# Fourier stage of a diffusion layer: four places for the prompt's output tiles, and the put-off sums, the first level's sums and the last level's halving at other places in the order

## The chip, the cores and the metric

The kernel runs on one core of a Trainium2 chip. The metric is the device time of one execution in microseconds. TensorE (PE) multiplies, VectorE (DVE), ScalarE (ACT) and GpSimd (POOL) do the elementwise work, and DMA transfers are issued from the queues of SyncE (SP) and GpSimd. The profile also gives the clock that TensorE was granted, as a share of full speed.

## The reference, cut to what matters

One layer of a diffusion backbone, in float32, for two streams: a prompt of 256 tokens and a latent of 2048 tokens, both with 1024 channels. The part that the change touches is the Fourier mixing of 512 of the projected channels, in four groups of 128:

```python
def project(h, w_in, q_g, k_g):
    p = h @ w_in
    q, k, v, f = jnp.split(p, [QK_WIDTH, 2 * QK_WIDTH, 2 * QK_WIDTH + ATTN_WIDTH], axis=-1)
    ...
    f = f.reshape(b, n, N_FOUR_GROUPS, FOUR_GROUP)
    return q, k, v, f

def fourier_mix(f, w_four):
    b, n, _, _ = f.shape
    spec = jnp.fft.fft2(f.astype(jnp.float32), axes=(1, 3), norm='ortho').real.astype(f.dtype)
    return jnp.einsum('bngc,gce->bnge', spec, w_four).reshape(b, n, FOUR_WIDTH)

def merge(attn, four, subln_g, lam_init, w_out):
    ...
    return jnp.concatenate([a.reshape(b, n, ATTN_WIDTH), four], axis=-1) @ w_out
```

Around it stand a normed and modulated projection, differential attention over 2560 keys, the output projection and a squared-ReLU MLP.

## The kernel before

The stages follow each other on one core: modulation vectors, the projection of all 18 token blocks (16 latent ones, two of the prompt), the Fourier stage, attention, output projection, MLP. The Fourier stage stands in the block `c2`, whose order of instructions is written out by hand (`tc.manual_schedule()`): each engine gets its instructions in the order in which the code issues them.

**How the transform is split.** Positions are 2048 rows. The projection already leaves sums and differences of row r and row r + 1024 in DRAM. The 2048-point transform is split by halves: the differences give the odd output columns (the level with the names E, DR and "o"), and the eight tiles `SS` of 128 rows hold the sums, 1024 rows. The level of 1024 folds these again: `diff` (L791) writes the difference of tile t and tile t + 4 to `d`, `summed` (L794) adds in place. Each set of differences is split into an even and an odd part by `even_odd`: two matmuls with a reversing matrix (`reverse`, L805 and L807) put the mirrored rows in PSUM, and VectorE writes `e` = d - mirror (L815) and `o` = d + mirror (L816); one row of the first `o` tile is overwritten by a copy (L818). Each product then takes half of the cosine or sine matrix. The same happens once more with 512 rows (`fold(512, t)`: L791, then L794), and the last 256 rows are halved by `s_last` (L781, L782).

**The levels and groups.** For each level the products run over the four channel groups g = 0 to 3: "o" (2048), then "p" (the prompt's 256 rows), "e" (1024), "f" (512) and "l" (256). Group g of a level makes two products A and B (`ab`, L744; `ab_half`, L752; for "o" `ab2048`, L732), each evacuated by ScalarE (L736 or L754). One group later `yT` multiplies A and B with the group's map: `py` (L698) and `pz` (L700) in PSUM, ScalarE copies py to `yu` (L704), and VectorE writes yu - pz and yu + pz to the output columns and their mirror image (L712, L713). Outputs of the latent stream gather in four tiles `ys` of 128 x 2048, one for each group (named ys_4656 to ys_4659 in the order below), stored by L773 after the last level; the prompt's go to tiles `yp` of 128 x 256, stored by L762. Both stores are issued from GpSimd's queue.

**The put-off sums.** At the 2048 level the output has a further split by parity: for group g, `yd` = u - v (L716) and u = u + v (L717) on VectorE, then four half-width results, two on GpSimd (L719, L720) and two on VectorE (L721, L722). Group 0 does this at once. For the groups 1 to 3 these six instructions are put in the list `LATE`, with copies of both products, and each `late()` issues those of the next group.

**The order.** The table `AFTER` says what is issued after group g of a level. PSUM tiles of the tag "y" (py, pz and rev) share three places, those of the tag "ab" five; a matmul that writes one waits for the readers of the tile that had the place before. `yp`, `d`, `yu` and `yd` come from the pool `f_t` with two or four places for a tag; `yp` has two. The pools are handed on tile by tile, so attention's first loads (keys L965, queries L993, values L971, all on SP's queue) go out as soon as the tiles of the Fourier stage that lay in their place are released.

Attention starts with score products (L1019), whose maxima VectorE takes (L1024) before ScalarE's exponentials. GpSimd starts it with a memset (L938), then scales and subtracts the two exponentials (L1058, L1059), which TensorE transposes (L1074).

Of the kernel before, what the change touches and what calls it, by code (L numbers as in the profile page):

```python
# [11 lines left out]
F32 = mybir.dt.float32  # L12
# [7 lines left out]
P = 128  # L20
D = 1024
KD = D // P
NP = 256
# [18 lines left out]
def body(tc, a, out):  # L42
    nc = tc.nc
    ctx = ExitStack()
    with ctx:
# [184 lines left out]
        with ExitStack() as c1:  # L230
# [357 lines left out]
            V = nc.vector  # L588
            with tc.manual_schedule():
# [12 lines left out]
                def ft32(pool, tag, nm, bufs):  # L602
                    return pool.tile([P, 512], F32, tag=tag, name=nm, bufs=bufs)
# [30 lines left out]
                SS = []  # L634
# [51 lines left out]
        with ExitStack() as c2:  # L686
            ft = c2.enter_context(tc.tile_pool(name="f_t", bufs=2, reuse_waits="tile"))
            yp = c2.enter_context(tc.tile_pool(name="f_y", bufs=1, reuse_waits="tile"))
            fw = c2.enter_context(tc.tile_pool(name="f_w", bufs=1, side="right", reuse_waits="tile"))
# [4 lines left out]
            def yT(dst, g, A, B, w, mirror_dst, parity=False):  # L694

                r = cw[g]
                py = pp.tile([P, 512], F32, tag="y", name="py", bufs=3)
                nc.tensor.matmul(py[:, :w], r[:, 0, :], A[:, :w], start=True, stop=True)  # L698
                pz = pp.tile([P, 512], F32, tag="y", name="pz", bufs=3)
                nc.tensor.matmul(pz[:, :w], r[:, 1, :], B[:, :w], start=True, stop=True)  # L700

                late = w == 512 and g > 0
                u, v = ft.tile([P, 512], F32, tag="yl" if late else "yu", name="yu", bufs=3 if late else 2)[:, :w], pz[:, :w]
                nc.scalar.copy(u, py[:, :w])  # L704
                if late:
                    v = ft.tile([P, 512], F32, tag="yv", name="yv", bufs=3)
                    nc.scalar.copy(v, pz)

                def go():
                    if not parity:  # L710
                        c = slice(1, P) if w == HW else slice(0, w)
                        V.tensor_sub(dst, u, v)  # L712
                        V.tensor_add(mirror_dst, u[:, c], v[:, c])  # L713
                        return
                    d = ft.tile([P, 512], F32, tag="yd", name="yd", bufs=2)
                    V.tensor_sub(d, u, v)  # L716
                    V.tensor_add(u, u, v)  # L717
                    de, do, se, so_ = d[:, 0:256], d[:, 256:512], u[:, 0:256], u[:, 256:512]
                    nc.gpsimd.tensor_add(dst[:, 0:256], de, do)  # L719
                    nc.gpsimd.tensor_sub(mirror_dst[:, 511:255:-1], de, do)  # L720
                    V.tensor_sub(dst[:, 511:255:-1], se, so_)  # L721
                    V.tensor_add(mirror_dst[:, 0:256], se, so_)  # L722

                LATE.append(go) if late else go()
# [32 lines left out]
            HW = P + 1  # L757

            def put_prompt(g, A, B):
                y = ft.tile([P, NP], F32, tag="yp", name=f"yp{g}")  # L760
                yT(y[:, 0:HW], g, A, B, HW, y[:, NP - 1:P:-1])
                nc.gpsimd.dma_start(four[g * P:g * P + P, 0:NP], y)  # L762

# [27 lines left out]
                V.tensor_sub(d[t], SS[t], SS[t + n // 2 // P])  # L791

            def summed(n, t):
                V.tensor_add(SS[t], SS[t], SS[t + n // 2 // P])  # L794

            def fold(n, t):
                diff(n, t)
                summed(n, t)
# [3 lines left out]
            def reverse(n, t):  # L802
                d, T = DD[n], n // P // 2
                REV[n, t] = ps = pp.tile([P, 512], F32, tag="y", name=f"rev{n}_{t}", bufs=3)
                nc.tensor.matmul(ps, jm, d[2 * T - 1 - t], start=True, stop=t == 0)  # L805
                if t:
                    nc.tensor.matmul(ps, k0, d[2 * T - t], start=False, stop=True)  # L807

            def even_odd(n, t):

                if (n, t) not in REV:
                    reverse(n, t)
                d, T, ps = DD[n], n // P // 2, REV.pop((n, t))
                e, o = (ft32(fa, "src", f"{x}{n}_{t}", 12) for x in "eo")
                V.tensor_sub(e, d[t], ps)  # L815
                V.tensor_add(o, d[t], ps)  # L816
                if t == 0:
                    nc.scalar.copy(o[0:1, :], d[T][0:1, :])  # L818
                for x, y in zip("eo", (e, o)):
                    EO.setdefault((n, x), []).append(y)  # L820

# [7 lines left out]
            def late():  # L829
                LATE.pop(0)()  # L830

            AFTER = {("o", 1): [(s_prompt,), (load_mats, "c1024", "s1024", "c512", "s512")],
                     ("o", 3): [(diff, 1024, 3), (diff, 1024, 2), (diff, 1024, 0), (diff, 1024, 1)],
                     ("p", 0): [(reverse, 512, 0), (even_odd, 512, 0)], ("p", 1): [(reverse, 512, 1), (even_odd, 512, 1)],
                     ("p", 3): [(summed, 1024, 0), (summed, 1024, 2)],
                     ("e", 0): [(summed, 1024, 1), (summed, 1024, 3), (fold, 512, 0)], ("e", 1): [(fold, 512, 1), (late,)],
                     ("e", 2): [(reverse, 256, 0), (s_last,), (late,)], ("e", 3): [(even_odd, 256, 0)],
                     ("f", 1): [(late,)]}

            def after(*at_):  # L840
                for fn, *args in AFTER.get(at_, ()):
# [7 lines left out]
            with tc.manual_schedule():  # L849
# [55 lines left out]
                for n, (ea, ma, eb, mb), w, p in (  # L905
                        ("p", (None, "c256", None, "s256"), HW, put_prompt),
                        ("e", (lambda: EO[512, "e"], "c1024", lambda: EO[512, "o"], "s1024"), 256, put(1024)),
                        ("f", (lambda: EO[256, "e"], "c512", lambda: EO[256, "o"], "s512"), 128, put(512)),
                        ("l", (None, "c256", None, "s256"), HW, put(256))):
                    for g in range(4):  # L910
                        if n in "pl":
                            nA, nB = (ab_half(g, q, (PR, S3)[n == "l"], MT[m][0], n) for q, m in enumerate((ma, mb)))
                        else:
                            nA = ab(g, 0, ea(), MT[ma], w, n)
                            nB = ab(g, 1, eb(), MT[mb], w, n)
                        last_put(*pend)
                        last_put, pend = p, (g, nA, nB)
                        if n == "p" and g == 0:
                            k_store(0, NK[0] // P - 1, parts[0])
                        if n == "e" and g == 0:  # L920
                            q_store(LAST, parts[1])
                        after(n, g)
# [8 lines left out]
        with ExitStack() as c3_:  # L931
# [265 lines left out]
            T = TSTEP  # L1197
# [692 lines left out]
        with ExitStack() as c6:  # L1890
# [52 lines left out]
            for i in range(7):  # L1943
                for k in range(16):
                    n = i * 16 + k
# [7 lines left out]
            with tc.manual_schedule():  # L1953
                pend, NM, loaded, KS = None, 7 * 24, 4, []
                for i in range(7):
                    for b in range(3):
                        ps = [pp.tile([P, 512], F32, tag="ps", name=f"ps{i}_{b}_{j}", bufs=6) for j in range(3)]
                        for k in range(16):
                            n, m = i * 16 + k, (i * 3 + b) * 8 + k // 2
# [35 lines left out]
                for j in range(3):  # L1995
                    t = 6 + j
# [70 lines left out]
```

## Time and profile before

| what | value |
|---|---|
| time, median of 3 runs | 2900.94 us (2899.92 to 2901.82) |
| profiled execution, its own time | 2899.16 us |
| its span in the trace | 2897.0 us |
| VectorE, share of the span | 69% |
| ScalarE | 53% |
| GpSimd | 36% |
| DMA traffic, mean | 170 GB/s |

Sums made from the trace are to be compared with the profiled execution's own time and not with the median. A row of a timeline gives the start, the duration of one instruction and its engine, line, operation and tiles (buffer numbers left out), and in brackets how long the engine was idle before and what ended that. Instructions alike and next to each other are put together (x2, x4), with their times together. Windows give the busy time of every engine in a stretch, then the clock granted to TensorE (1.00 is full speed) and the share and rate of the DMA engines.

### The profile page before, as it was taken

The page shows a single profiled execution, that of the slowest core. Times are in us where ns is not written, and L with a number is a line of the kernel's source. Part 1 is how long each engine was busy: PE and PEld are TensorE (multiplying, and loading weights), DVE is VectorE, ACT ScalarE, POOL GpSimd, SP SyncE. Part 2 cuts the span into 40 slices and gives each one's busy share as a digit, 9 for nine tenths or more (in the row PEclk, how much of TensorE's full clock was granted, in tenths as well). Part 3 has the DMA queues.
Part 4 walks back from the last instruction along what each step waited for, and adds up shares of the span by engine and source line. Part 5 has one row for each costly group of instructions (what it writes and reads, how often), then busy time and mean ns, then how long its engine had stood idle before and what let it go on. Part 6 is the DMA issues. An engine that isn't in the chain of part 4 may idle for free.

```text
span 2897.0 us, 43205 instructions
## 1 busy us (share of the span) xinstructions
PE 2850.3 (98%) x15119; PEld 2470.4 (85%) x15119; DVE 2011.4 (69%) x3377; ACT 1547.0 (53%) x3504; POOL 1057.0 (36%) x866
## 2 busy tenths in 40 slices
PE   8999999799999999999999999999999999999999
PEld 4888788588888888888889999999998888888887
DVE  6667776798988988964477777778775354345554
ACT  4333323598998989953356565556554332233221
POOL 1112112499998999942213333333332000000000
PEclk9999999999999999999999999999999999999999
DMA  7777888420121202136777677667657464445663
GB/s 282 206 201 189 229 214 228 182 102 28 48 110 44 104 30 74 60 101 200 225 240 227 210 254 230 213 230 233 225 178 251 139 200 138 138 142 180 201 207 109
DMA packets 392779, 492.93 MB, mean 170 GB/s; under 512 B 26467, under 2 KB 306384, under 8 KB 389490
## 3 DMA queue, kind: packets, MB, share of 16 engines
q1 hardware_dynamic: 387136, 479.73, 52.4%
q0 software_dynamic: 1872, 7.28, 0.8%
q10 hardware_dynamic: 3554, 3.17, 0.4%
q8 instruction: 119, 1.95, 0.3%
q14 instruction: 98, 0.80, 0.1%
HBM read 312.58 MB, written 179.59 MB: 170 GB/s over the span
## 4 chain that ended last, share of the span: by engine, by line
PE 89%; DVE 4%; DMA 3%; ACT 2%; issue 1%; POOL 1%; SPq 0%; ACTq 0%; DVEq 0%; POOLq 0%
PE Ss L1019 10%; PE ps L88 8%; PE ps L89 8%; PE ps L90 8%; PE pts L1074 5%; PE po L90 4%; PE po L88 4%; PE po L89 4%; PE pj L88 4%; PE pj L89 4%; PE pj L90 4%; PE pA L1682 2%; PE pA L1683 2%; PE pB L1683 2%; PE pB L1682 2%; PE pB L1684 2%
## 5 line engine op out<-in xcount | busy, mean ns | idle before, releaser
L1024 DVE TENSOR_REDUCE mxs<-Ss 128x1 f32<-128x512 f32 x636 | 413.0, 684 | 64.7 <-PE Ss L1019 52.9
L1359 DVE TENSOR_TENSOR sl<-sr,sh 128x768 fp32r<-128x768 f32 x168 | 161.7, 963 | 338.0 <-ACT sh L1358 336.4
L1059 POOL TENSOR_TENSOR P0s<-P0s,P1s 128x1024 f32<-128x1024 f32 (+2 forms) x128 | 378.5, 2957 | 10.7
L1358 ACT CAST sh<-sr 128x768 fp32r<-128x768 f32 x168 | 140.2, 835 | 424.8 <-PE ps L89 422.0
L1724 POOL TENSOR_TENSOR gs<-g,g 128x384 f32<-128x384 f32 x48 | 69.6, 1451 | 469.5 <-ACT g L1694 399.9
L1043 ACT ACTIVATE P1s<-Ss,mxs 128x512 f32<-128x512 f32 x318 | 215.2, 694 | 36.4 <-DVE mxs L1027 35.4
L88 PE MATMUL pj<-wh,hh 128*128 128x512 f32 x576 | 228.9, 397 | 4.5 <-DVE qn L289 3.9
L89 PE MATMUL ps<-tlT,sh 128*128 128x512 f32 x585 | 229.3, 392 | 0.0
L88 PE MATMUL ps<-thT,sh 128*128 128x512 f32 x585 | 229.0, 391 | 0.0
L89 PE MATMUL pj<-wl,hh 128*128 128x512 f32 x576 | 227.4, 395 | 0.5 <-DVE wl L524 0.5
L90 PE MATMUL ps<-thT,sl 128*128 128x512 f32 x585 | 227.7, 389 | 0.0
L90 PE MATMUL pj<-wh,hl 128*128 128x512 f32 x576 | 226.7, 394 | 0.0
L1043 ACT ACTIVATE P0s<-Ss,mxs 128x512 f32<-128x512 f32 x318 | 214.1, 691 | 5.5 <-DVE mxs L1027 4.8
L1019 PE MATMUL Ss<-KS1s,Qs 128*128 128x512 f32 x636 | 195.9, 420 | 5.0 <-ACT P0s L1043 2.4
L1019 PE MATMUL Ss<-KS0s,Qs 128*128 128x512 f32 x636 | 196.8, 422 | 2.4 <-ACT P1s L1043 2.4
L1074 PEld LDWEIGHTS pts<-ident,P0s 128*128 128x128 f32 x1280 | 158.2, 140 | 44.2 <-POOL P0s L1059 1.4
L1074 PE MATMUL pts<-ident,P0s 128*128 128x128 f32 x1280 | 191.3, 273 | 1.9 <-POOL P0s L1059 1.2
L1693 ACT ACTIVATE g<-uz 128x384 f32<-128x384 f32 x144 | 75.8, 527 | 201.6 <-DVE uz L1716 171.4
L1058 POOL TENSOR_SCALAR P1s<-P1s,tots 128x1024 f32<-128x1024 f32 (+2 forms) x128 | 171.8, 1342 | 5.8
L1086 DVE TENSOR_TENSOR als<-pts,ahs 128x512 fp32r<-128x512 f32 x256 | 165.8, 680 | 6.9 <-ACT ahs L1081 6.6
L88 PE MATMUL ps<-ophT,sh 128*128 128x512 f32 x423 | 165.8, 392 | 1.1 <-DVE uz L1716 1.1
L90 PE MATMUL ps<-ophT,sl 128*128 128x512 f32 x423 | 165.7, 392 | 0.0
(530 smaller groups left out, 8055.7 us busy)
## 6 DMA issues: line engine op xcount, KB each, us to landing
sr<-sd SPq DMA_DIRECT2D x84, 768.0 KB
a<-in_w SPq DMA_DIRECT2D x184, 256.0 KB
sd<-gs SPq DMA_DIRECT2D x192, 192.0 KB
sd<-g SPq DMA_DIRECT2D x144, 192.0 KB
wm<-in_w_mod SPq DMA_DIRECT2D x32, 512.0 KB
Qs<-qd SPq DMA_DIRECT2D x32, 512.0 KB
b<-in_w SPq DMA_DIRECT2D x64, 256.0 KB
b<-tsum SPq DMA_DIRECT2D x64, 256.0 KB
```

The source lines that it names most:

```text
L88: nc.tensor.matmul(ps, lh, rh, start=first, stop=False)
L89: nc.tensor.matmul(ps, lh, rl, start=False, stop=False)
L90: nc.tensor.matmul(ps, ll, rh, start=False, stop=last)
L1019: nc.tensor.matmul(S[:, :w], self.Q[:, x, m, j * P:j * P + P], self.hd.KS[m][:, b * 512:b * 512 + w], start=(x == 0), stop=(x == 1))
L1024: nc.vector.tensor_reduce(self.mx[j][:, m, b:b + 1], self.S[j, m, b], axis=AX.X, op=ALU.max)
L1043: nc.scalar.activation(dst, S, AF.Exp, bias=self.mx[j][:, m, 6:7], accum_out=self.sm[j][:, m, b:b + 1])
L1058: nc.gpsimd.tensor_scalar(p, p, tot[:, 3:4], 0.0, op0=ALU.mult, op1=ALU.add)
L1059: nc.gpsimd.tensor_add(d, d, p)
L1074: nc.tensor.transpose(pt[:, c:c + P], self.p0[j][:, (kb + t) * P:(kb + t + 1) * P], ident)
L1086: nc.vector.tensor_sub(t, self.pt[kb], f32(self.A[kb][0]))
L1358: nc.scalar.copy(hi, src)
L1359: nc.vector.tensor_sub(lo, src, f32(hi))
```

## The change

It has five parts. The prompt's output tiles `yp` come from the pool `f_w`, on the other side of SBUF, with four places for two. The four sums of the level of 1024 (L794) go to GpSimd and are all issued after the last group of "o", behind the four differences, whose order changes from tiles 3, 2, 0, 1 to 3, 2, 1, 0. The copy of one row into the first `o` tile of a level (L818) goes from ScalarE to VectorE. The put-off sums move: that of group 1 from after ("e", 1) to after ("o", 3), that of group 2 from ("e", 2) to ("p", 2), that of group 3 from ("f", 1) to ("l", 2). The folds of 512 move from ("e", 0) and ("e", 1) to ("p", 3) and ("e", 0), in the order 1, 0, and the reversal, the even and odd parts of 256 rows come after ("e", 1) and the last level's halving alone after ("e", 2). From L838 on all line numbers are 2 lower. What is computed stays the same.

```diff
--- before.py
+++ after.py
@@ -757,7 +757,7 @@
             HW = P + 1
 
             def put_prompt(g, A, B):
-                y = ft.tile([P, NP], F32, tag="yp", name=f"yp{g}")
+                y = fw.tile([P, NP], F32, tag="yp", name=f"yp{g}", bufs=4)
                 yT(y[:, 0:HW], g, A, B, HW, y[:, NP - 1:P:-1])
                 nc.gpsimd.dma_start(four[g * P:g * P + P, 0:NP], y)
 
@@ -791,7 +791,7 @@
                 V.tensor_sub(d[t], SS[t], SS[t + n // 2 // P])
 
             def summed(n, t):
-                V.tensor_add(SS[t], SS[t], SS[t + n // 2 // P])
+                (nc.gpsimd if n == 1024 else V).tensor_add(SS[t], SS[t], SS[t + n // 2 // P])
 
             def fold(n, t):
                 diff(n, t)
@@ -815,7 +815,7 @@
                 V.tensor_sub(e, d[t], ps)
                 V.tensor_add(o, d[t], ps)
                 if t == 0:
-                    nc.scalar.copy(o[0:1, :], d[T][0:1, :])
+                    V.tensor_copy(o[0:1, :], d[T][0:1, :])
                 for x, y in zip("eo", (e, o)):
                     EO.setdefault((n, x), []).append(y)
 
@@ -830,12 +830,10 @@
                 LATE.pop(0)()
 
             AFTER = {("o", 1): [(s_prompt,), (load_mats, "c1024", "s1024", "c512", "s512")],
-                     ("o", 3): [(diff, 1024, 3), (diff, 1024, 2), (diff, 1024, 0), (diff, 1024, 1)],
+                     ("o", 3): [(diff, 1024, 3), (diff, 1024, 2), (diff, 1024, 1), (diff, 1024, 0)] + [(summed, 1024, t) for t in (3, 1, 2, 0)] + [(late,)],
                      ("p", 0): [(reverse, 512, 0), (even_odd, 512, 0)], ("p", 1): [(reverse, 512, 1), (even_odd, 512, 1)],
-                     ("p", 3): [(summed, 1024, 0), (summed, 1024, 2)],
-                     ("e", 0): [(summed, 1024, 1), (summed, 1024, 3), (fold, 512, 0)], ("e", 1): [(fold, 512, 1), (late,)],
-                     ("e", 2): [(reverse, 256, 0), (s_last,), (late,)], ("e", 3): [(even_odd, 256, 0)],
-                     ("f", 1): [(late,)]}
+                     ("p", 2): [(late,)], ("p", 3): [(fold, 512, 1)], ("e", 0): [(fold, 512, 0)],
+                     ("e", 1): [(reverse, 256, 0), (even_odd, 256, 0)], ("e", 2): [(s_last,)], ("l", 2): [(late,)]}
 
             def after(*at_):
                 for fn, *args in AFTER.get(at_, ()):
```

VectorE where the 2048 level ends and the prompt's level begins (d_3 to d_0: first-level differences; yd, yu: the put-off sum of group 1; e_0, o_0: first even and odd parts; yp: a prompt tile). Before:

```order
L791 TENSOR_TENSOR d_3_4667<-ss_4544,ss_4550 128x512
L791 TENSOR_TENSOR d_2_4666<-ss_4544,ss_4550 128x512
L791 TENSOR_TENSOR d_0_4664<-ss_4541,ss_4547 128x512
L791 TENSOR_TENSOR d_1_4665<-ss_4541,ss_4547 128x512
L815 TENSOR_TENSOR e_0_4837<-d_0_4664,rev_0_4835 128x512
L816 TENSOR_TENSOR o_0_4838<-d_0_4664,rev_0_4835 128x512
L712 TENSOR_TENSOR yp_4852<-yu,pz 128x129
```

and of the change:

```order
L791 TENSOR_TENSOR d_1_4665<-ss_4541,ss_4547 128x512
L791 TENSOR_TENSOR d_0_4664<-ss_4541,ss_4547 128x512
L716 TENSOR_TENSOR yd<-yu,yv 128x512
L717 TENSOR_TENSOR yu<-yu,yv 128x512
L721 TENSOR_TENSOR ys_4657<-yu 128x256
L722 TENSOR_TENSOR ys_4657<-yu 128x256
L815 TENSOR_TENSOR e_0_4848<-d_0_4664,rev_0_4846 128x512
L816 TENSOR_TENSOR o_0_4849<-d_0_4664,rev_0_4846 128x512
L818 COPY o_0_4849<-d_2_4666 1x512
L712 TENSOR_TENSOR yp_4863<-yu,pz 128x129
```

The four instructions of the put-off sum of group 1 now stand ahead of the first even and odd parts, and the row copy behind them.

GpSimd at the same place (ss: the sequence tiles that are summed, two tiles under one name). Before:

```order
L762 DMA four<-yp_4852 128x256
L762 DMA four<-yp_4879 128x256
L762 DMA four<-yp_4899 128x256
L762 DMA four<-yp_4921 128x256
L719 TENSOR_TENSOR ys_4657<-yd 128x256
L720 TENSOR_TENSOR ys_4657<-yd 128x256
```

and of the change, where the first two rows stand a second time ahead of those shown:

```order
L794 TENSOR_TENSOR ss_4544<-ss_4544,ss_4550 128x512
L794 TENSOR_TENSOR ss_4541<-ss_4541,ss_4547 128x512
L719 TENSOR_TENSOR ys_4657<-yd 128x256
L720 TENSOR_TENSOR ys_4657<-yd 128x256
L762 DMA four<-yp_4863 128x256
L762 DMA four<-yp_4890 128x256
```

Four sums stand ahead of its part of the first put-off sum, and that now ahead of the prompt's stores.

VectorE at the end of the stage, in the last level's third and fourth group. One piece of the difference:

```order
 L712 TENSOR_TENSOR ys_4657<-yu,pz 128x129
 L713 TENSOR_TENSOR ys_4657<-yu,pz 128x127
+L716 TENSOR_TENSOR yd<-yu,yv 128x512
+L717 TENSOR_TENSOR yu<-yu,yv 128x512
+L721 TENSOR_TENSOR ys_4659<-yu 128x256
+L722 TENSOR_TENSOR ys_4659<-yu 128x256
 L712 TENSOR_TENSOR ys_4658<-yu,pz 128x129
 L713 TENSOR_TENSOR ys_4658<-yu,pz 128x127
```

The last put-off sum stands ahead of the last two groups' outputs. On GpSimd its two instructions (L719, L720) stand between the second and the third of the stores L773.

## The prediction

> **What bounds the kernel now.** I read the page first, for the engine that sets the end, then the timeline of TensorE over the Fourier stage, then VectorE and GpSimd there.
>
> ```profile
> span 2897.0 us, 43205 instructions
> PE 2850.3 (98%) x15119; PEld 2470.4 (85%) x15119; DVE 2011.4 (69%) x3377; ACT 1547.0 (53%) x3504; POOL 1057.0 (36%) x866
> PE   8999999799999999999999999999999999999999
> ```
>
> TensorE is busy for 98% of the span. The one slice at 7 tenths is the eighth (507 to 579 us): the second half of the Fourier stage and the start of attention, the place of every edit. Attention behind it keeps TensorE at 9 tenths, so a microsecond won here should pass to the end, and one lost too. TensorE's timeline there:
>
> ```profile
> 502.24 0.39 PE L700 MATMUL pz<-abp,cw 128*128 128x129 f32 x2
> 502.66 1.13 PE L805 MATMUL rev<-d,jm 128*128 128x512 f32 x2
> 509.33 1.03 PE L744 MATMUL pabe<-c,e 128*128 128x256 f32 x4
> 510.20 1.03 PE L744 MATMUL pabe<-s,o 128*128 128x256 f32 x4
> 512.39 0.67 PE L698 MATMUL py<-abe,cw 128*128 128x256 f32 x2 [1.17 <-DVE yp L713]
> 517.93 1.12 PE L805 MATMUL rev<-d,jm 128*128 128x512 f32 x2 [1.84 <-DVE d L791]
> 522.76 0.70 PE L700 MATMUL pz<-abe,cw 128*128 128x256 f32 x2 [1.55 <-DVE ys L713]
> 528.43 0.79 PE L744 MATMUL pabf<-c,e 128*128 128x128 f32 x2 [4.97 <-DVE e L815]
> 529.67 0.79 PE L744 MATMUL pabf<-s,o 128*128 128x128 f32 x2 [0.45 <-ACT o L818]
> 538.17 0.49 PE L700 MATMUL pz<-abf,cw 128*128 128x128 f32 x2 [0.97 <-DVE ys L713]
> 542.82 0.49 PE L700 MATMUL pz<-abl,cw 128*128 128x129 f32 x2
> ```
>
> The brackets are the waits: 1.17 + 1.84 + 1.55 + 4.97 + 0.45 + 0.97 = 10.95 us, all behind VectorE but the 0.45 behind ScalarE's row copy. A bracket counts from the modelled end of the matmul before. The two groups of four at 509.33 and 510.20 start 0.87 apart and take 1.03, so the next could have started 0.16 before that end; six waits cost about 1.0 more. The windows show a further loss (columns: stretch, length, busy time of PE, PEld, DVE, ACT and POOL, clock, DMA):
>
> ```profile
> 515.00:520.00 5.00, 3.16 (x14) 2.07 (x13) 4.82 (x9) 0.79 (x3) 0.66 (x1) 1.00 0.18 69
> 525.00:528.00 3.00, 0.00 (x0) 0.00 (x0) 2.97 (x6) 0.00 (x0) 1.59 (x2) 0.50 0.79 307
> 528.00:531.00 3.00, 2.13 (x6) 1.74 (x7) 0.96 (x2) 1.04 (x3) 0.00 (x0) 0.50 0.98 423
> 531.00:534.00 3.00, 3.00 (x13) 2.73 (x13) 1.10 (x3) 1.17 (x4) 0.00 (x0) 0.50 0.47 163
> 534.00:537.00 3.00, 3.00 (x26) 3.00 (x25) 2.93 (x6) 1.69 (x7) 1.79 (x2) 0.89 0.03 5
> ```
>
> The wait of 4.97 halved the granted clock (0.50) until some 534.5 us; the wait of 1.84 did not (1.00). Work at half clock loses half its time: 0.5 x 3.00 + 0.11 x 3.00 = 1.8 us, and with the 2.13 busy of 528 to 531, 2.9; between these I take 2.3. TensorE so loses 10.95 + 1.0 + 2.3 = 14.25 us.
>
> Why VectorE was late, and where it ends:
>
> ```profile
> 495.69 2.49 DVE L791 TENSOR_TENSOR d<-ss,ss 128x512 f32<-128x512 f32 x4
> 505.29 0.68 DVE L816 TENSOR_TENSOR o<-d,rev 128x512 f32<-128x512 f32 x1
> 511.76 0.29 DVE L712 TENSOR_TENSOR yp<-yu,pz 128x129 f32<-128x129 f32 x1 [5.18 <-ACT abe L736]
> 512.16 1.29 DVE L794 TENSOR_TENSOR ss<-ss,ss 128x512 f32<-128x512 f32 x2
> 534.44 0.69 DVE L716 TENSOR_TENSOR yd<-yu,yv 128x512 f32<-128x512 f32 x1
> 537.51 0.37 DVE L712 TENSOR_TENSOR ys<-yu,pz 128x128 f32<-128x128 f32 x1
> 541.68 0.39 DVE L713 TENSOR_TENSOR ys<-yu,pz 128x127 f32<-128x127 f32 x1
> 543.65 0.41 DVE L713 TENSOR_TENSOR ys<-yu,pz 128x127 f32<-128x127 f32 x1
> 504.55 7.09 DMA four<-yp
> ```
>
> The last row is from the chain of waits: the store of the first prompt tile lands at 511.64. The third prompt tile needs that buffer, one of two, so VectorE stood 5.18 us (the ScalarE name is an inference; it had long been done). From then on it has no pause until 529 us, and TensorE waits for it again and again.
>
> **The change part by part.** *Four prompt tiles* take the 5.18 away. *The sums on GpSimd* take four adds of 0.6 (two in 1.29) from VectorE; *the row copy* leaves ScalarE's queue, where the copies of the f products stood behind it, for VectorE. A one-row copy is not in VectorE's rows here; it costs between nothing and the 0.68 of the o row, I take 0.4. *The put-off sums* of groups 1 and 2 and the 256-level reversal come earlier. So VectorE has in the e and f levels little left to be late with: I forecast all six waits gone but for 0.6 us before the 256-level reversal (its bracket 1.84 less the 1.3 of sums that stood in front of it).
>
> In their place stands a new wait, at the second reversal of the 512 level (502.66 now). It needs the PSUM bank whose reader is o of tile 0. In front of that e and o now stand four put-off instructions, and GpSimd runs its four sums beside them. Do the two engines hinder each other?
>
> ```profile
> 491.37 0.73 POOL L719 TENSOR_TENSOR ys<-yd 128x256 f32<-128x256 f32 x1 [11.18 <-DVE yd L716]
> 492.04 0.43 DVE L721 TENSOR_TENSOR ys<-yu 128x256 f32<-128x256 f32 x1
> 519.30 0.69 DVE L717 TENSOR_TENSOR yu<-yu,yv 128x512 f32<-128x512 f32 x1
> 519.34 1.24 POOL L719 TENSOR_TENSOR ys<-yd 128x256 f32<-128x256 f32 x1 [4.66 <-DVE yd L716]
> 520.03 0.83 DVE L721 TENSOR_TENSOR ys<-yu 128x256 f32<-128x256 f32 x1
> L1086 DVE TENSOR_TENSOR als<-pts,ahs 128x512 fp32r<-128x512 f32 x256 | 165.8, 680 | 6.9 <-ACT ahs L1081 6.6
> L1561 POOL TENSOR_TENSOR ht<-hTb 128x512 f32<-128x512 f32 x8 | 10.3, 1288 | 0.0
> L1559 POOL TENSOR_TENSOR ht<-hTb,hTb 128x512 f32<-128x512 f32 x8 | 13.3, 1669 | 38.1 <-ACT hTb L224 24.2 <-DMA xo<-in_x_sample 13.9
> ```
>
> They do, by turns. L719 alone takes 0.73, beside L717 1.24: it gets through 0.59 after L717 ends (519.99 to 520.58). L721 alone takes 0.43, beside L719 0.83, and ends 0.28 after it (520.86 against 520.58). VectorE with both inputs in SBUF and GpSimd wait for each other's end. L1086 with one input in PSUM keeps 680 ns through attention.
>
> The Trainium skill, SBUF — State Buffer, "Who interferes with whom", says this of a VectorE instruction with two SBUF inputs against a GpSimd one that reads SBUF: whichever comes second stands until the first is through. It speaks against this change; by it the sum is the one worked out below, without it the first rival's. The trace agrees (L721, 0.43 and 0.83).
>
> A sum of 128x512 costs 1.28 to 1.67 by the last two rows; I lay 1.2 of holding (1.28 less the overlap of some 0.08) for each. From 495.69, in the new order: two differences to 496.89; sum to 498.09; two differences to 499.29; sum to 500.5; L716 to 501.1; sum to 502.3; L717 to 502.9; sum to 504.1; L721 0.35, L719 0.65, L722 0.35 to 505.45; e and o to 506.7. The reversal starts near 506.85 instead of 502.66: **4.2 us lost**. TensorE then idles 4.3 us or so, nearer to the 4.97 that halved the clock than to the 1.84 that did not, so I charge a halving again, 2.3. The ends of the range: 0 for the wait and the clock if the sums hold nothing back; 1.6 more for the wait at 1.67 a sum, and 2.2 more if the clock stays halved 9 us as it did from 525 to 534 (4.5).
>
> The Trainium skill, TensorE: Matmul & The Clock Gate, "What's actually happening", puts the drop after one idle window of about 3.4 us. By it the halving comes as charged. Here only the two waits above show it.
>
> TensorE: 14.25 - 4.2 - 0.6 - 2.3 = **7.15 us won**; its last Fourier matmul ends at 543.31 - 7.15 = 536.2.
>
> *Group 3's put-off sum* moves to the last level's third group. Its four instructions take 537.51 - 534.44 = 3.07. The second group's L713 now ends at 542.07, 1.24 before TensorE's last. From there 3.07, then four short ones of some 0.9: VectorE ends 3.07 + 0.9 - 1.24 = 2.7 behind TensorE, where it is 544.06 - 543.31 = 0.75 today. Attention's first exponential waits for VectorE's maxima, which stand behind: **1.95 us lost**.
>
> *The gate of the first GpSimd product:*
>
> ```profile
> 555.88 0.10 POOL L938 MEMSET P_first<- 128x1 f32 x1 [10.76 <-DMA four<-ys]
> 554.21 0.17 DVE L1049 RECIPROCAL tots<-tots 128x1 f32<-128x1 f32 x1
> 569.89 0.55 PE L1074 MATMUL pts<-ident,P0s 128*128 128x128 f32 x3 [1.23 <-POOL P0s L1059]
> 506.03 0.32 SPq L993 DMA_DIRECT2D Qs<-qd  x1
> ```
>
> GpSimd waits for the last of four output stores, 1.5 us after its data (554.38), and TensorE later 1.23 for GpSimd. In the new order two stores go out ahead of the put-off sum, so two instead of four queue at the end. Between 0 and 1.23 I take **0.9 won**.
>
> The sum: -7.15 + 1.95 - 0.9 = **-6.1 us**. It stands against the profiled execution's 2899.16 (its span 2897.0 and 2.16 around it), which is 1.78 below the median of 2900.94: **2894.8 us** beside that median.
>
> **The rivals.** *Free sums* (chance 0.18): the engines do not hold each other there, or the clock stays up. With neither wait nor halving -6.1 - 4.2 - 2.3 = -12.6, with one of them about -9: 2888.3 to 2892. For: GpSimd's copies are short and the turns may fall well. Against: L721.
>
> *The loss travels* (0.12): sums at 1.67 and a clock halved for 9 us, -6.1 + 1.6 + 2.2 = -2.3: 2898.6. For: after 528.43 it did stay halved through two busy windows.
>
> *Late queries* (0.12), the slower side. The first query tile (506.03, SP queue) lies where the first-level differences lay, and their order is changed, so another tile may hold the place. It costs nothing while it lands before 536; one with other transfers about takes up to 12 us (GpSimd's store wait of 10.76). From an issue later than 524 each microsecond is lost. If the place came free only with the stage's end, 536, the tile would land at 547: +11 - 6.1 = +4.9, and with the clock halved once more (2.3) +7.2: 2908. For: today it is issued just as VectorE's second o ends (505.29 + 0.68 = 505.97), so it does wait for such a place. Against: the differences are dead after the 256-level copy, near 521.
>
> *Nothing moves* (0.02): another transfer sets attention's start; 2900.9.
>
> **How the numbers follow.** The forecast has 0.56; its own range is 2892 to 2897.5. About 0.2% (5.8 us) is what a measurement here tells from no change; the forecast lies just beyond, so I put 0.44 of its 0.56 on faster and 0.12 within. Faster 0.44 + 0.18 = 0.62; within 0.12 + 0.12 + 0.02 = 0.26; slower 0.12. The range of 8 in 10 is 2889 to 2900: the free sums' end (2888.3) and most of late queries left out.
>
> **What would show it.** Right: no wait of VectorE between the prompt tiles; one TensorE wait of about 4 us at the second L805 and a half clock after it; L794 on GpSimd in turn with L716 and L717; no wait at L744; VectorE's last Fourier instruction 2 to 3 us behind TensorE's. Wrong: L716 at 0.69 beside L794 (free sums), a wait of the first L1019 for the query load (late queries), or a gain here that is gone by 600 us.

## The result and the profile after

The changed kernel takes 2893.73 us (median of 14 runs, 2891.38 to 2896.37), the kernel before 2901.24 us (14 runs): a ratio of 0.9973, 95% interval 0.9965 to 0.9981, or 7.5 us less. Forecast were 2894.8 us in a range of 2889 to 2900.

The page of the changed kernel: span, busy times, TensorE's slices.

```profile
span 2889.3 us, 43207 instructions
PE 2850.0 (99%) x15119; PEld 2471.2 (86%) x15119; DVE 2013.4 (70%) x3375; ACT 1546.3 (54%) x3502; POOL 1062.9 (37%) x870
PE   8999999899999999999999999999999999999999
```

The busy time of TensorE is what it was (2850.3 before); the eighth slice went from 7 to 8 tenths, and of the 7.7 us of span that are gone 7.4 were idle time of TensorE (46.7 before, 39.3 after). TensorE's timeline in the changed kernel, from the end of the prompt's first output to attention:

```profile
501.62 0.39 PE L700 MATMUL pz<-abp,cw 128*128 128x129 f32 x2
505.50 1.68 PE L805 MATMUL rev<-d,jm 128*128 128x512 f32 x2 [3.49 <-DVE o L816]
511.68 1.03 PE L744 MATMUL pabe<-c,e 128*128 128x256 f32 x4
522.49 0.38 PE L744 MATMUL pabf<-c,e 128*128 128x128 f32 x2
532.38 0.49 PE L700 MATMUL pz<-abl,cw 128*128 128x129 f32 x2
535.75 1.20 PE L1017 MATMUL Ss<-KS1s,Qs 128*128 128x512 f32 x4 [0.55 <-DVE ys L713]
539.69 1.89 PE L1017 MATMUL Ss<-KS1s,Qs 128*128 128x512 f32 x4 [2.28 <-ACT P0s L1041]
571.87 0.36 PE L88 MATMUL po<-ahs,Vs 128*128 128x256 f32 x1
```

All six brackets of the kernel before are gone, and one of 3.49 at the second reversal is new. In attention's first products TensorE now waits 0.55 and 2.28, where it waited 0.97 before. The windows around the wait of 3.49 (columns as before: busy times of PE, PEld, DVE, ACT, POOL, then the clock):

```profile
500.00:505.00 5.00, 2.01 (x14) 1.50 (x12) 4.86 (x6) 1.21 (x4) 4.83 (x4) 1.00 0.74 143
505.00:508.50 3.50, 3.00 (x4) 1.29 (x5) 1.25 (x4) 0.00 (x0) 0.57 (x1) 0.63 1.06 242
508.50:512.00 3.50, 3.50 (x27) 3.29 (x26) 2.63 (x6) 1.51 (x6) 0.58 (x2) 0.88 0.92 361
```

The clock falls behind the wait (0.63, 0.88) and is whole from 512 to the stage's end; the half clock of 524 to 534.5 in the kernel before is gone. In attention it falls once more: behind the wait of 2.28 it is 0.50 from 541 to 543, where the kernel before has 1.00 from 543 to 575. VectorE and GpSimd around the second reversal, and VectorE's last output:

```profile
495.07 3.56 DVE L791 TENSOR_TENSOR d<-ss,ss 128x512 f32<-128x512 f32 x4
495.84 1.64 POOL L794 TENSOR_TENSOR ss<-ss,ss 128x512 f32<-128x512 f32 x1 [0.25 <-DVE d L791]
498.11 4.99 POOL L794 TENSOR_TENSOR ss<-ss,ss 128x512 f32<-128x512 f32 x3 [0.63 <-DVE d L791]
498.56 1.75 DVE L716 TENSOR_TENSOR yd<-yu,yv 128x512 f32<-128x512 f32 x1
500.41 1.57 DVE L717 TENSOR_TENSOR yu<-yu,yv 128x512 f32<-128x512 f32 x1
504.77 0.68 DVE L816 TENSOR_TENSOR o<-d,rev 128x512 f32<-128x512 f32 x1
514.10 0.28 DVE L712 TENSOR_TENSOR yp<-yu,pz 128x129 f32<-128x129 f32 x1
535.31 0.38 DVE L713 TENSOR_TENSOR ys<-yu,pz 128x127 f32<-128x127 f32 x1
```

The four differences take 3.56 for 2.49, L716 and L717 take 1.75 and 1.57 for 0.69: the engines go by turns. The third prompt tile (514.10) starts without a wait.

**A measure for the experiments.** Programs that are alike up to the place of the change start their first difference (L791) anywhere between 493.92 and 496.83 us; a spread that runs of one kernel show too (2897.07 to 2903.31 us for the kernel before in one series). From attention's first product with V (L88) to the end all thirteen profiles take 2316.8 to 2317.6 us. So the experiments are compared by what lies between, called the **stretch** here. Before it runs from 495.69 to the row

```profile
579.99 0.36 PE L88 MATMUL po<-ahs,Vs 128*128 128x256 f32 x1
```

that is 84.30 us, and in the change from 495.07 to 571.87, 76.80 us: 7.50 less, the whole difference of the medians. Nothing is given back later. Each stretch is read from one profiled execution. Parts that two kernels have alike agree well (33.45 and 33.46, 36.68 twice, 37.80 and 37.75 in the table below), but how far a stretch varies from execution to execution was not measured. The stretch splits at the end of TensorE's last Fourier matmul (L700): up to there 47.62 before (543.31 - 495.69) and 37.80 after (532.87 - 495.07), 9.82 less; from there to L88 36.68 before and 39.00 after, 2.32 more.

### The profile page after: what moved, and what is told of

It is laid out like the page before. It is cut to its first block, busy times and chain, and to the rows that moved or that the text cites. A ratio compares the mean times of both kernels' runs of the same rounds, so it can differ in the third digit from the quotient of the medians.

```text
span 2889.3 us, 43207 instructions
## 1 busy us (share of the span) xinstructions
PE 2850.0 (99%) x15119; PEld 2471.2 (86%) x15119; DVE 2013.4 (70%) x3375; ACT 1546.3 (54%) x3502; POOL 1062.9 (37%) x870
## 3 DMA queue, kind: packets, MB, share of 16 engines
q8 instruction: 119, 1.95, 0.3%
## 4 chain that ended last, share of the span: by engine, by line
PE 90%; DVE 4%; ACT 2%; DMA 2%; POOL 1%; issue 1%; SPq 0%; ACTq 0%; DVEq 0%; POOLq 0%
PE Ss L1017 11%; PE ps L88 8%; PE ps L89 8%; PE ps L90 8%; PE pts L1072 5%; PE po L90 4%; PE po L88 4%; PE po L89 4%; PE pj L89 4%; PE pj L88 4%; PE pj L90 4%; PE pA L1680 2%; PE pA L1681 2%; PE pB L1680 2%; PE pB L1681 2%; PE pB L1682 2%
## 5 line engine op out<-in xcount | busy, mean ns | idle before, releaser
L88 PE MATMUL pj<-wh,hh 128*128 128x512 f32 x576 | 228.6, 397 | 2.5 <-DVE qn L289 1.8
L88 PE MATMUL ps<-thT,sh 128*128 128x512 f32 x585 | 229.0, 391 | 0.0
L88 PE MATMUL ps<-ophT,sh 128*128 128x512 f32 x423 | 165.7, 392 | 1.1 <-DVE uz L1714 1.1
```

The lines of the kernel that those rows point to most:

```text
L88: nc.tensor.matmul(ps, lh, rh, start=first, stop=False)
```

## The experiments

All in one table; "L700" and "rest" are the two parts of the stretch. The ratio is to runs of the kernel before on the same chip, whose medians in the four series were 2900.67 to 2902.03 us.

| kernel | stretch | L700 | rest | median us | ratio (95%) |
|---|---|---|---|---|---|
| before | 84.30 | 47.62 | 36.68 | 2901.24 | |
| the change | 76.80 | 37.80 | 39.00 | 2893.73 | 0.9973 (0.9965 to 0.9981) |
| before, four prompt places | 80.75 | 44.07 | 36.68 | 2895.47 | 0.9979 (0.9970 to 0.9988) |
| before, sums on GpSimd | 87.77 | 49.61 | 38.16 | 2904.14 | 1.0009 (1.0000 to 1.0017) |
| change, sums on VectorE | 72.86 | 33.45 | 39.41 | 2888.66 | 0.9953 (0.9941 to 0.9966) |
| change, two prompt places | 76.67 | 37.59 | 39.08 | 2891.46 | 0.9965 (0.9953 to 0.9978) |
| change, reversals elsewhere in PSUM | 72.76 | 33.79 | 38.97 | 2888.86 | 0.9956 (0.9944 to 0.9969) |
| sums on VectorE, last sum in pieces | 69.74 | 33.46 | 36.28 | 2885.75 | 0.9944 (0.9931 to 0.9958) |
| change, wait filled | 75.19 | 36.12 | 39.07 | 2891.27 | 0.9965 (0.9952 to 0.9977) |
| before, wait filled | 82.47 | 45.76 | 36.71 | 2898.52 | 0.9989 (0.9980 to 0.9998) |
| change, row copy on ScalarE | 76.44 | 37.75 | 38.69 | 2892.36 | 0.9971 (0.9959 to 0.9982) |
| sums on VectorE, two places | 79.04 | 38.41 | 40.63 | 2893.57 | 0.9974 (0.9964 to 0.9984) |
| pieces, reversals elsewhere | 69.48 | 32.66 | 36.82 | 2885.49 | 0.9948 (0.9935 to 0.9960) |

**Before with four prompt places.**

```diff
-y = ft.tile([P, NP], F32, tag="yp", name=f"yp{g}")
+y = fw.tile([P, NP], F32, tag="yp", name=f"yp{g}", bufs=4)
```

> The kernel before with one part of the change alone: four places for the prompt tiles. Theory (VectorE's load bounds the e and f levels, the stall of 5.18 us is only a part of its lateness): the stall goes, the waits of 1.17 and 1.84 go, but the wait ahead of the f products stays at 3 to 6 us because sums, folds and put-off sums stand as before; TensorE's last Fourier matmul 2 to 5 us earlier, time 3 to 5 us below before. Rival A (the stall is the whole cause): the wait ahead of the f products goes too, 8 to 10 us below before, as much as the full change or more. Rival B (the stall only moves to the next wait): within 1 us of before.

The stretch is 3.55 shorter, the medians differ by 5.85, somewhat more than the theory's 3 to 5. Its timeline of TensorE still has the wait ahead of the f products:

```profile
518.44 0.70 PE L700 MATMUL pz<-abe,cw 128*128 128x256 f32 x2 [1.50 <-DVE ys L713]
524.11 0.80 PE L744 MATMUL pabf<-c,e 128*128 128x128 f32 x2 [4.97 <-DVE e L815]
```

The waits of 1.17 and 1.84 are gone, that of 4.97 is as long as it was: the stall was not its cause. Rival A is out.

**Before with the sums on GpSimd**, where they stood.

```diff
-V.tensor_add(SS[t], SS[t], SS[t + n // 2 // P])
+(nc.gpsimd if n == 1024 else V).tensor_add(SS[t], SS[t], SS[t + n // 2 // P])
```

> The kernel before with one part of the change alone: the four sums of the level of 1024 on GpSimd, at the places where they stood. Theory (VectorE with two inputs in SBUF and GpSimd stand for each other, and a sum on GpSimd takes 1.28 to 1.67 us for 0.6 on VectorE): the sums run beside L791, L794 and the put-off sums and hold VectorE about as long as they last; time 1 to 3 us above before. Rival (VectorE is unloaded by four adds of 0.6): 2 us below before.

The stretch is 3.47 longer, and the median 2.8; the interval of the ratio just reaches 1. On VectorE and GpSimd of that kernel:

```profile
515.84 3.29 DVE L794 TENSOR_TENSOR ss<-ss,ss 128x512 f32<-128x512 f32 x1
516.08 2.49 POOL L794 TENSOR_TENSOR ss<-ss,ss 128x512 f32<-128x512 f32 x2
```

One sum of VectorE, 0.69 elsewhere, stands 3.29 beside two sums of GpSimd that together take 2.49, and TensorE's wait at the 256-level reversal grows from 1.84 to 4.23. Alone, this part of the change is a loss. Up to L700 it is 1.99; the other 1.48 lie in attention, where TensorE's waits are as in the kernel before (0.97 and 1.22 for 0.97 and 1.23) but the clock falls earlier (0.74 from 570 to 575, 1.00 there before). That this clock is the sums' doing isn't shown.

**The change with the sums on VectorE**, at the same place in the order (the last diff undone).

> The changed kernel with the four sums back on VectorE, at the same place (after the fourth group of the 2048 level). Theory (by turns): L716 and L717 take 0.6 to 0.7 us instead of 1.75 and 1.57, e and o of tile 0 come about 2.4 us earlier though VectorE now does the four adds itself; the wait of 3.49 at the second reversal falls to 1.0 to 1.5, the clock isn't halved behind it; TensorE's Fourier stage ends 2.5 to 5 us earlier, time 2 to 5 us below the change (9 to 13 below before). Rival (GpSimd takes load off VectorE): VectorE is 2.4 us later, the wait grows to 5 to 6 us, time 2 to 4 us above the change.

The stretch is 3.94 shorter than in the change. VectorE and TensorE there:

```profile
495.27 2.49 DVE L791 TENSOR_TENSOR d<-ss,ss 128x512 f32<-128x512 f32 x4
500.08 0.69 DVE L716 TENSOR_TENSOR yd<-yu,yv 128x512 f32<-128x512 f32 x1
502.35 1.13 PE L805 MATMUL rev<-d,jm 128*128 128x512 f32 x2
503.84 0.68 DVE L816 TENSOR_TENSOR o<-d,rev 128x512 f32<-128x512 f32 x1
```

L716 is back at 0.69, and VectorE, which now makes the four sums itself, is through with o of tile 0 at 504.52, 9.25 after its first difference against 10.38 in the change (505.45 - 495.07). But the second reversal starts at 502.35, ahead of that o. It no longer waits for it at all: it has another place in PSUM. So the time was as the theory said, but the wait of 1.0 to 1.5 that it left in place is gone altogether. The engines' turns and the place in PSUM changed together here; the kernel with the reversals elsewhere, further down, changes the place alone.

**The change with two prompt places** (the first diff undone).

> The changed kernel with the prompt tiles back to two places. Theory (the stall comes back, but in the new order VectorE has less left to be late with): VectorE waits some 4 to 5 us for the store of the first tile, one TensorE wait of 2 to 3 us comes at the reversal of 256 rows; time 2 to 4 us above the change (4 to 6 below before). Rival A (the places bring all of the gain): as slow as before. Rival B (the new order leaves room for the stall): within 1 us of the change.

The stretch is the same within 0.13. The medians differ by 2.3; the profiled executions differ by 1.85, of which 1.15 lies ahead of the first difference. GpSimd's first prompt store and VectorE's third prompt tile:

```profile
505.44 0.57 POOL L762 DMA_DIRECT2D four<-yp  x1 [1.75 <-DVE yp L713]
512.74 0.28 DVE L712 TENSOR_TENSOR yp<-yu,pz 128x129 f32<-128x129 f32 x1
```

There is no stall: 7.3 us lie between the two, and the store takes 6.0 here (7.09 before). The theory, that a stall comes back, was wrong, rival B right.

**The change with the reversals' PSUM tiles from the products' tag.**

```diff
-REV[n, t] = ps = pp.tile([P, 512], F32, tag="y", name=f"rev{n}_{t}", bufs=3)
+REV[n, t] = ps = pab(f"r{n}_{t}")
```

> The changed kernel, sums on GpSimd, but the reversals' PSUM tiles taken from the tag of the products (ab, five places) and not from that of py and pz (three). In the change the second reversal waits 3.49 us for o of tile 0 (its place); in the kernel with the sums on VectorE the same matmul started 0.90 us ahead of its e (502.35 against 503.25), so it had another place. Measure: the stretch from the first L791 to attention's first L88, 84.30 us before, 76.80 in the change, 72.86 with the sums on VectorE. Theory (the place makes most of the wait, the turns of the engines 1.1 us of it): wait at the second reversal under 0.3, no halved clock, stretch 73.0 to 74.5, time 2.5 to 4 us below the change. Rival (the turns alone make it): TensorE waits 2 to 3.5 us one step later, at the first e products (L744), with the clock halved there, stretch 75.5 to 77.

VectorE and TensorE there (the reversals' tiles are named pabr):

```profile
500.32 1.75 DVE L716 TENSOR_TENSOR yd<-yu,yv 128x512 f32<-128x512 f32 x1
503.61 1.02 PE L805 MATMUL pabr<-d,jm 128*128 128x512 f32 x2
506.54 0.67 DVE L816 TENSOR_TENSOR o<-d,pabr 128x512 f32<-128x512 f32 x1
```

The engines go by turns as before (1.75), o of tile 0 is as late as in the change (507.21, 10.38 after 496.83), but the reversal starts 6.78 after the first difference for 10.43, without a wait. The stretch is 4.04 shorter, as short as with the sums on VectorE. So with another place the turns cost TensorE next to nothing: the price was paid because the second reversal had the PSUM place of the first.

**The last put-off sum in four pieces**, sums on VectorE.

```diff
-... ("l", 2): [(late,)]}
+... ("f", 2): [(late,), (piece,)], ("f", 3): [(piece,)], ("l", 0): [(piece,)], ("l", 1): [(piece,)]}
...
+PIECES.extend(((dif, gp1, gp2), (add,), (v1,), (v2,))) if g == 3 else [f() for f in (dif, add, gp1, gp2, v1, v2)]
```

> The changed kernel with the sums on VectorE, and the last put-off sum (group 3) not in one piece after the last level's third group but in four pieces (L716 with L719 and L720; L717; L721; L722) after the f groups 2 and 3 and the l groups 0 and 1, where VectorE pauses 0.26 to 0.71 us a group. Theory (the put-off sum in one piece makes VectorE end 2.8 us behind TensorE, and attention's first exponential waits for it): VectorE's last L713 ends 0.5 to 0.9 us after TensorE's last L700, TensorE gains no new wait over 0.5 us, stretch 70.0 to 71.0, time 2 to 3 us below the kernel with the sums on VectorE (2885.5 to 2887). Rival (attention's start is set by the query and key loads or by GpSimd behind the stores): less than 0.7 us.

The ends of TensorE's and VectorE's Fourier work there:

```profile
527.33 0.49 PE L700 MATMUL pz<-abl,cw 128*128 128x129 f32 x2
528.16 0.41 DVE L713 TENSOR_TENSOR ys<-yu,pz 128x127 f32<-128x127 f32 x1
```

and a window in attention:

```profile
537.00:540.00 3.00, 3.00 (x11) 1.27 (x9) 2.59 (x7) 3.00 (x11) 0.00 (x0) 1.00 1.00 380
```

VectorE ends 0.75 behind TensorE for 2.82, and the stretch is 3.12 shorter than in the kernel with the sums on VectorE. About 2.1 of that is the tail itself. The rest fits the clock: in the kernel with the sum in one piece the same window, behind TensorE's wait of 2.28 in attention, reads

```profile
537.00:540.00 3.00, 3.00 (x9) 2.37 (x9) 2.30 (x6) 2.87 (x9) 0.00 (x0) 0.54 1.00 421
```

**The waits filled** with matmuls whose product isn't read: four ahead of the second reversal of the change, five ahead of the first f products of the kernel before.

```diff
+def fill(k):
+    ps = pab("x")
+    for _ in range(k):
+        nc.tensor.matmul(ps, jm, d1024[3], start=True, stop=True)
...
-... ("p", 1): [(reverse, 512, 1), ...
+... ("p", 1): [(fill, 4), (reverse, 512, 1), ...
```

> The changed kernel with four matmuls added ahead of the second reversal (each 0.86 us at full clock, product of a first-level difference with the reversing matrix, never read), in the time in which TensorE waits 3.49 us. Theory (the idle time halves the clock, which costs 1.8 us behind the wait): granted clock 1.00 from 500 to 512, the second reversal starts as late as before after the first L791 (10.4 us) within 0.3, the stretch 1.3 to 2.3 us shorter than 76.80, time 1 to 2.5 us below the change. Rival (the halving comes from the load on the chip and not from the idle time, or the fillers push the reversal back): no gain, within 0.5 us or slower.

> The kernel before with five matmuls added ahead of the first f products (L744), in the time in which TensorE waits 4.97 us. Theory (that wait halves the clock for some 9 us): clock 1.00 from 524 to 535 and the stretch (84.30) shorter by the clock's share of the old loss, which the prediction set at 2.3 and the balance of the change puts at 3.1: 2.3 to 3.3 us, time as much below before. Rival (the clock falls anyway, because of the waits of 1.84 and 1.55 ahead of it): under 1 us.

The change filled, its timeline of TensorE (the added matmuls are L832) and the window behind the wait:

```profile
503.44 3.60 PE L832 MATMUL pabx<-d,jm 128*128 128x512 f32 x8
507.10 1.12 PE L805 MATMUL rev<-d,jm 128*128 128x512 f32 x2
```

```profile
505.00:508.50 3.50, 3.44 (x9) 1.26 (x8) 2.85 (x6) 0.00 (x0) 1.75 (x3) 1.00 1.02 187
```

The kernel before filled, TensorE:

```profile
523.62 4.46 PE L832 MATMUL pabx<-d,jm 128*128 128x512 f32 x10
528.76 0.49 PE L744 MATMUL pabf<-c,e 128*128 128x128 f32 x2 [0.69 <-DVE e L815]
530.00 0.49 PE L744 MATMUL pabf<-s,o 128*128 128x128 f32 x2 [0.75 <-ACT o L818]
536.60 0.49 PE L700 MATMUL pz<-abf,cw 128*128 128x128 f32 x2 [1.19 <-DVE ys L713]
```

In the change the reversal is as late as without the matmuls (10.44 after the first difference), the clock stays at 1.00, and the stretch is 1.61 shorter: more work, less time. In the kernel before the clock stays at 1.00 too (520 to 535), and the gain is 1.83 in the stretch, under the 2.3 to 3.3 of the theory and over the rival's 1; the medians differ by 3.5. A part of what the clock gives is lost again to VectorE: the later wait grows from 0.97 to 1.19, the row copy's from 0.45 to 0.75.

**The row copy on ScalarE**, all else as in the change.

```diff
-V.tensor_copy(o[0:1, :], d[T][0:1, :])
+nc.scalar.copy(o[0:1, :], d[T][0:1, :])
```

> The changed kernel with the copy of one row (L818) back on ScalarE. Stretch 76.80 us in the change. Theory (the copy takes VectorE 0.41 twice; at the first one the second reversal waits for o, at the second the prompt's and e outputs have 0.2 to 0.7 us of pauses behind them; on ScalarE it stands ahead of evacuations that wait for TensorE anyway): within 0.5 us of 76.80 either way. Rival (as in the kernel before the f products wait for the row copy, 0.45): a wait of 0.4 to 0.8 at the f or e products that read o, stretch 77.2 to 78.

The stretch is 0.36 shorter, and there is no new wait at the products that read o. Where the copy stands makes no difference that these runs show.

**Sums on VectorE with two prompt places.**

```diff
-(nc.gpsimd if n == 1024 else V).tensor_add(SS[t], SS[t], SS[t + n // 2 // P])
+V.tensor_add(SS[t], SS[t], SS[t + n // 2 // P])
...
-y = fw.tile([P, NP], F32, tag="yp", name=f"yp{g}", bufs=4)
+y = ft.tile([P, NP], F32, tag="yp", name=f"yp{g}")
```

> The changed kernel with the sums on VectorE and only two places for the prompt tiles; the stretch is 72.86 with four. Theory (in the change two places cost nothing because the wait at the second reversal puts 7.3 us between the first prompt store and the third tile, and the store takes 6.5 to 7.1; without that wait the gap is 4.3 us, 505.66 to 509.94): VectorE stands 2.0 to 3.5 us at the third prompt tile, TensorE waits 1 to 3 us, stretch 74 to 76.5, time 1.5 to 4 us above the kernel with four. Rival (the new order needs no third place): within 0.5 us of 72.86.

The first prompt store on GpSimd, the third tile on VectorE, and TensorE's first output matmul of the e level:

```profile
506.02 0.57 POOL L762 DMA_DIRECT2D four<-yp  x1 [2.61 <-DVE yp L713]
513.62 0.29 DVE L712 TENSOR_TENSOR yp<-yu,pz 128x129 f32<-128x129 f32 x1 [3.24 <-DMA four<-yp]
514.25 0.67 PE L698 MATMUL py<-abe,cw 128*128 128x256 f32 x2 [2.75 <-DVE yp L713]
```

The stall is as forecast (3.24), its price higher: 6.18 in the stretch, 4.9 in the medians, not 1.5 to 4. TensorE waits 2.75 and 0.53, and the clock halves behind these (0.63 from 515 to 518). So the four places are worth 6 us in this kernel and nothing in the change, where the wait at the second reversal had already put 7.3 us between the first store and the third tile.

**All together**: the kernel with the pieces, and its reversals from the products' tag.

```diff
-REV[n, t] = ps = pp.tile([P, 512], F32, tag="y", name=f"rev{n}_{t}", bufs=3)
+REV[n, t] = ps = pab(f"r{n}_{t}")
```

> Four prompt places, the new order, sums on VectorE, the last put-off sum in four pieces and the reversals' PSUM tiles from the products' tag. The pieces alone gave a stretch of 69.73. Theory (the waits left in the Fourier stage, 0.18 at the 256-level reversal and 0.1 to 0.4 at the prompt's py and pz, come from the three places of py and pz): 0.3 to 0.9 us less, stretch 68.8 to 69.4. Rival (they come from VectorE's load): within 0.2 us of 69.73.

The stretch is 0.26 shorter than with the pieces alone, below the theory's 0.3 to 0.9 and near the rival's 0.2: up to L700 0.80 is won, 0.54 of it is lost in attention. It can't be told from the kernel with the pieces; both are faster than the kernel before and than the change, by some 15 to 16 and 8 us.

## Why the prediction was right

| term | forecast | measured |
|---|---|---|
| old loss of TensorE in the stage | -14.25 | -14.17 |
| new wait at the second reversal | +4.2 | +2.67 net |
| half clock behind it | +2.3 | +1.68 |
| wait ahead of the 256-level reversal | +0.6 | none |
| sum up to L700 | -7.15 | -9.82 |
| last put-off sum's tail | +1.95 | +2.07 |
| GpSimd's gate | -0.9 | -0.15 |
| sum up to L88 | -6.1 | -7.50 |

The measured terms leave 0.4 of the 2.32 behind L700 unassigned; it lies in attention's first products.

The total came out 1.4 from the forecast partly by luck. Up to L700 the forecast had 2.67 us too little won, behind it 1.27 too little lost, and these errors partly cancel.

**The old loss.** With the products' order of the change and its tag for the reversals, the shortest time from the first difference to the last L700 is 33.45 us (sums on VectorE) and 33.46 (pieces), with small waits left. The kernel before stood 47.62 - 33.45 = 14.17 over it; the sum of brackets, restarts and clock had 14.25. Against the last kernel, whose reversals lie elsewhere, it is 47.62 - 32.66 = 14.96. That the waits travel was not borne out: none of the six came back.

**The new wait** came at the named matmul, for the named reason (the place whose reader is o of tile 0), and the forecast's working for o was 11.0 us after the first difference where 10.38 were measured. The reversal starts 3.46 later than before (10.43 against 6.97) and not 4.2. Up to L700 the change without the halving (wait filled) is 36.12 - 33.45 = 2.67 over the best of these: of the 3.46 some 0.8 comes back. The kernel with the sums on VectorE has small waits, such as 0.18 at the 256-level reversal, that don't arise behind the large one. What the prediction did not see is how much hung on the place. It took the place as given and priced the turns; taking away the place took the whole wait (4.04 with its clock) and left the turns as they were. What the turns add where the place is kept is an estimate: o is done 10.38 after the first difference with them and 9.25 without, so they make some 1.1 of the 3.49, and the work put ahead of o makes the rest. No run has that place with the sums on VectorE, and why the reversal got another one there isn't shown. The Trainium skill, SBUF — State Buffer, "Who interferes with whom", told the turns rightly (L716 at 1.75 beside a GpSimd sum of 1.64, 0.69 without). What the turns cost TensorE hung on a queue of PSUM places.

**The clock** was halved as forecast; it cost 37.80 - 36.12 = 1.68, not 2.3.

**The tail**: VectorE ends 2.82 behind TensorE (535.69 against 532.87), 0.75 before; 2.7 were forecast. The prediction had no clock behind the tail. The kernel with the pieces shows that the tail cost still more, 3.12 with the clock in attention, which stays whole there without the wait of 2.28.

**The gate** is the step that failed. "Two instead of four queue at the end" did not come true, and next to nothing was won. GpSimd's last two stores, then VectorE, GpSimd and TensorE at the start of attention:

```profile
535.76 1.10 POOL L773 DMA_DIRECT2D four<-ys  x2 [1.38 <-DVE ys L713]
546.22 0.17 DVE L1047 RECIPROCAL tots<-tots 128x1 f32<-128x1 f32 x1
547.74 0.10 POOL L936 MEMSET P_first<- 128x1 f32 x1 [10.89 <-DMA four<-ys]
561.77 0.55 PE L1072 MATMUL pts<-ident,P0s 128*128 128x128 f32 x3 [1.09 <-POOL P0s L1057]
```

a window between the stores' issue and the memset, and the stores' row in the view of the DMA queues (instructions, KB of each, median time from issue to landing):

```profile
537.00:540.00 3.00, 0.72 (x3) 0.30 (x2) 2.97 (x7) 1.14 (x3) 0.00 (x0) 1.00 0.97 324
```

```profile
four<-ys POOLq DMA_DIRECT2D x4, 1024.0 KB, 8.5
```

The memset still comes 1.35 behind the reciprocal (1.50 before), and TensorE waits 1.09 for 1.23. The first two stores are issued at 530.83 and 532.17, 4.9 and 3.6 us ahead of the last two; before it was 2.7 and 1.4. But they take 5.3 and 7.9 us to land, so both are still under way when the third goes out at 535.76. The last one lands 11.4 us after its issue, 11.2 before; meanwhile the DMA engines are busy for 97%, with these stores and attention's loads. How much would be won without that gate was not tried.

**The rivals.** Free sums: the turns were there, so its premise fell, but with the reversals elsewhere in PSUM its time came out (2888.86). The loss travels: no. Nothing moves: no, 7.5 us are won. Late queries: the first half came true, the load is issued 14 us later,

```profile
520.24 0.32 SPq L991 DMA_DIRECT2D Qs<-qd  x1
532.62 2.57 PE L1017 MATMUL Ss<-KS0s,Qs 128*128 128x512 f32 x10
```

and the first score product at 532.62 doesn't wait for it: the 12 us between are enough.

**Which part did it?** Mostly the order. Places alone win 3.55 of the 7.50, sums on GpSimd alone lose 3.47, the row copy moves nothing, and with two places and all else of the change 7.63 are there. But the parts aren't apart: without the wait at the second reversal the two places cost 6.18, and the order with the row copy, two places and the sums on VectorE wins 84.30 - 79.04 = 5.26.

## What to carry to other kernels

A wait that an edit makes may hide a second one: test a part together with the others beside which it is to stay, since the same four buffers were worth 0 or 6 us. Where a stall is charged to a slow engine, look at which buffer the waiting instruction was given; another place may cost nothing while the engine stays slow. A put-off piece of work is best cut so small that each piece fits in a pause of its engine, since one block at a stage's end delays the next stage's first step and, by idle time, its clock.

## What the runs showed of the hardware that was not expected

The clock was halved after less than full idleness. In the kernel with two places and the sums on VectorE:

```profile
512.00:515.00 3.00, 0.75 (x4) 0.68 (x4) 1.35 (x4) 0.04 (x1) 0.56 (x1) 1.00 0.71 295
515.00:518.00 3.00, 2.47 (x5) 1.09 (x4) 2.96 (x8) 0.33 (x1) 0.54 (x1) 0.63 0.24 87
```

TensorE's longest wait there was 2.75 us, and it worked 0.75 of the 3 us ahead of the drop. In the change the clock fell to 0.50 (541 to 543) behind attention's wait of 2.28, with 0.72 of 3 us worked from 537 to 540. The Trainium skill, TensorE: Matmul & The Clock Gate, "What's actually happening", speaks of an idle window of about 3.4 us; here a part-idle one was enough. And unneeded matmuls in such a wait made both kernels faster, by 1.6 and 1.8 us.
